# Column mean of an 8192 x 8192 matrix: other transfer sizes at both ends of the load stream, and a new assignment of PSUM banks

## Chip, cores, metric

One core of one Trainium2 chip. The metric is device time in microseconds (us), as the median of several executions; lower is better.

## The reference

```python
def setup_inputs():
    return {"x": np.random.randn(8192, 8192).astype(np.float32)}

def reference(x):
    return np.mean(x, axis=0)      # 8192 column means
```

The input is 268.4 MB of float32, the output 32 KB.

## The kernel before

The 8192 rows are 64 *slabs* of 128 rows, one row per partition. A transfer issued by GpSimd brings a slab from device memory and casts it to bfloat16 on the way. TensorE sums its 128 rows by multiplying with a column of ones, 512 columns (a *chunk*) per matmul, so 16 matmuls per slab, accumulating over all slabs in PSUM. At the end ScalarE (even chunks) and VectorE (odd chunks) multiply a finished chunk by 1/8192 and move it to a result row in SBUF (a *drain*), and the result row is stored.

Which bank a chunk accumulates in:

```python
    n_chunks = 16;  n_q = 2;  BANKS = 8;  QROWS = (0, 32, 64, 96)   # values for this shape
    def chunk_psum(c):
        b, q = c // n_q, c % n_q          # chunks 0,1 in bank 0; 2,3 in bank 1; ...
        return acc[QROWS[q] : QROWS[q] + 1, b * CHUNK : b * CHUNK + cw]
```

How the loads are cut. Slabs 0 to 59 come as 15 groups of four, slabs 60, 61 and 62 singly, and the last slab in nine narrow pieces. Groups and singles share two buffers of four slabs each; the last slab has one of its own.

```python
    slab_pool = tc.tile_pool(name="slab", bufs=2)
    bulk = n_slabs - 1
    # groups: (0,4) (4,4) ... (56,4), then (60,1) (61,1) (62,1)
    for g0, ns in groups:
        slab = slab_pool.tile([P, SPD * C], MM_DT)
        nc.gpsimd.dma_start(out=slab..., in_=x[g0 * P : (g0 + ns) * P, :]...)
        # 16 matmuls for each of the ns slabs
    ...
    last = slab_pool.tile([P, C], MM_DT)
    # pieces: [0,1] [2,3] ... [12,13] [14] [15]
    for pi, cs in enumerate(pieces):
        nc.gpsimd.dma_start(out=last[:, p0:pend], in_=row[:, p0:pend])
        # a matmul for each chunk of the piece, then its drain
        nc.sync.dma_start(out=out[p0:pend], in_=res[0:1, p0:pend])
```

The text above is the order in which the program is written. A scheduler, when the program is built, decides the order in which each engine issues its instructions, and the built order differs from it.

Of the kernel before, what the change touches and what calls it, by code (L numbers as in the profile page):

```python
# [1 line left out]

# [4 lines left out]



@with_exitstack  # L10
def kernel(
    ctx: ExitStack,
    tc: tile.TileContext,
    x: bass.AP,
    out: bass.AP,
):
    nc = tc.nc
    P = nc.NUM_PARTITIONS
    R, C = x.shape
    assert R % P == 0, "row count must be a multiple of 128"  # L20
    n_slabs = R // P

    MM_DT = mybir.dt.bfloat16
    CHUNK = 512
    BANKS = 8
    QROWS = (0, 32, 64, 96)
    n_chunks = (C + CHUNK - 1) // CHUNK
    n_q = (n_chunks + BANKS - 1) // BANKS
    assert n_q <= len(QROWS), "input too wide for a single pass"
    inv_r = 1.0 / float(R)  # L30

    const_pool = ctx.enter_context(tc.tile_pool(name="const", bufs=1))
    slab_pool = ctx.enter_context(tc.tile_pool(name="slab", bufs=2))
    psum_pool = ctx.enter_context(tc.tile_pool(name="acc", bufs=1, space=bass.MemoryType.PSUM))
    res_pool = ctx.enter_context(tc.tile_pool(name="res", bufs=1))

    ones_f32 = const_pool.tile([P, 1], mybir.dt.float32)
    nc.vector.memset(ones_f32, 1.0)  # L38
    ones = const_pool.tile([P, 1], MM_DT)
    nc.scalar.copy(out=ones, in_=ones_f32)  # L40

    acc = psum_pool.tile([P, BANKS * CHUNK], mybir.dt.float32)
    res = res_pool.tile([1, C], mybir.dt.float32)

    def chunk_psum(c):
        b, q = c // n_q, c % n_q
        cw = min(CHUNK, C - c * CHUNK)
        return acc[QROWS[q] : QROWS[q] + 1, b * CHUNK : b * CHUNK + cw]

    def chunk_cols(c):  # L50
        cw = min(CHUNK, C - c * CHUNK)
        return c * CHUNK, cw

    SPD = max(1, min(4, (8 << 20) // (P * C * 2)))
    TAIL_SINGLES = 3

    bulk = n_slabs - 1
    groups = []
    s0 = 0
    while s0 < max(0, bulk - TAIL_SINGLES):  # L60
        ns = min(SPD, bulk - TAIL_SINGLES - s0)
        groups.append((s0, ns))
        s0 += ns
    while s0 < bulk:
        groups.append((s0, 1))
        s0 += 1

    for g0, ns in groups:
        slab = slab_pool.tile([P, SPD * C], MM_DT)
        src = x[g0 * P : (g0 + ns) * P, :]  # L70
        if ns > 1:
            nc.gpsimd.dma_start(  # L72
                out=slab[:, : ns * C].rearrange("p (k c) -> p k c", c=C),
                in_=src.rearrange("(k p) c -> p k c", p=P),
            )
        else:
            nc.gpsimd.dma_start(out=slab[:, :C], in_=src)  # L77
        for k in range(ns):
            s = g0 + k
            for c in range(n_chunks):  # L80
                c0, cw = chunk_cols(c)
                nc.tensor.matmul(  # L82
                    out=chunk_psum(c),
                    lhsT=ones,
                    rhs=slab[:, k * C + c0 : k * C + c0 + cw],
                    start=(s == 0),
                    stop=False,
                )

    s = n_slabs - 1  # L90
    last = slab_pool.tile([P, C], MM_DT)
    row = x[s * P : (s + 1) * P, :]
    pieces = []
    for b in range(BANKS):
        cs = [c for c in range(b * n_q, min((b + 1) * n_q, n_chunks))]
        if not cs:
            continue
        if b == BANKS - 1 or (b + 1) * n_q >= n_chunks:
            pieces.extend([[c] for c in cs])
        else:  # L100
            pieces.append(cs)

    for pi, cs in enumerate(pieces):
        p0, _ = chunk_cols(cs[0])
        pend = chunk_cols(cs[-1])[0] + chunk_cols(cs[-1])[1]
        nc.gpsimd.dma_start(out=last[:, p0:pend], in_=row[:, p0:pend])  # L106
        for c in cs:
            c0, cw = chunk_cols(c)
            nc.tensor.matmul(  # L109
                out=chunk_psum(c),  # L110
                lhsT=ones,
                rhs=last[:, c0 : c0 + cw],
                start=(s == 0),
                stop=True,
            )
        for c in cs:
            c0, cw = chunk_cols(c)
            src_ap = chunk_psum(c)
            dst_ap = res[0:1, c0 : c0 + cw]
            if c % 2 == 0:  # L120
                nc.scalar.mul(out=dst_ap, in_=src_ap, mul=inv_r)  # L121
            else:
                nc.vector.tensor_scalar(  # L123
                    out=dst_ap,
                    in0=src_ap,
                    scalar1=inv_r,
                    scalar2=None,
                    op0=mybir.AluOpType.mult,
                )
        nc.sync.dma_start(out=out[p0:pend], in_=res[0:1, p0:pend])  # L130


# [1 line left out]
_INS = ['x']  # L134
_OUTS = [((8192,), 'float32')]


# [23 lines left out]
```

## Time and profile before

| | before |
|---|---|
| median time | 637.47 us (636.98 to 637.87, 5 runs) |
| span of the profiled execution | 635.0 us |
| TensorE busy | 148.7 us, 23% |
| device memory read | 268.44 MB, 423 GB/s over the span |
| last whole slab has landed | 623.4 us |
| from there to the end | 11.6 us |

First the profile page of the kernel before: the busy time of the engines, and the DMA and throughput rows of the table that cuts the span into 40 slices. A digit is the mean busy share of the 16 DMA engines in tenths; GB/s counts the bfloat16 bytes written, so device memory is read at twice that.

```profile
PE 148.7 (23%) x1024; PEld 51.4 (8%) x1024; DVE 4.9 (1%) x9; ACT 5.4 (1%) x10; POOL 17.8 (3%) x31
...
DMA  8999999999999999999999999999999999999992
GB/s 178 219 215 215 215 215 219 220 219 218 215 215 215 216 220 220 220 215 215 215 215 220 218 220 218 215 215 215 216 220 221 218 216 215 215 215 217 211 217 59
```

The loads keep the DMA engines busy from the first slice to the last but one, and no compute engine is near full. Only the ends are open to question, above all the last slice, where the rate falls to 59 GB/s.

Now the timeline of the kernel before near its end: start, duration, engine, source line, operation, output and input, how many merged; in brackets the idle time ahead and what ended it. First what GpSimd (POOL) issues; L77 is a whole slab, L106 a narrow piece of the last slab.

```profile
556.41 0.54 POOL L77 DMA_DIRECT2D slab<-in_x_dram  x1 [37.38 <-PE acc L82]
556.94 3.20 POOL L106 DMA_DIRECT2D last<-in_x_dram  x6
585.88 0.53 POOL L106 DMA_DIRECT2D last<-in_x_dram  x1 [25.74 <-DMA slab<-in_x_dram]
595.79 0.53 POOL L77 DMA_DIRECT2D slab<-in_x_dram  x1 [9.38 <-DMA slab<-in_x_dram]
597.50 0.53 POOL L77 DMA_DIRECT2D slab<-in_x_dram  x1 [1.18 <-PE acc L82]
598.03 0.53 POOL L106 DMA_DIRECT2D last<-in_x_dram  x1
599.33 0.53 POOL L106 DMA_DIRECT2D last<-in_x_dram  x1 [0.77 <-DMA last<-in_x_dram]
```

Seven of the nine narrow pieces are issued ahead of the last two whole slabs. The first of those two, by the view, waited last for the landing of the slab before it, the second for TensorE to give back a buffer (L77 waits for L82). The waits for a landing come from the built program, which hands its loads eight semaphores in turn: with eight loads under way, GpSimd issues the next one only when an earlier one has landed.

So seven narrow pieces land early (the seventh at 604.0 us), and a whole slab lands near the end, at 623.4 us. The page gives the median time from issue to landing of the two narrow pieces behind it:

```profile
last<-in_x_dram POOLq DMA_DIRECT2D x2, 128.0 KB, 25.7
```

The rest of that timeline, from that slab's landing on (weight loads left out):

```profile
623.43 3.31 PE L82 MATMUL acc<-slab,ones 128*1 128x512 bf16 x16 [6.10 <-DMA slab<-in_x_dram]
...
626.58 1.89 PE L109 MATMUL acc<-last,ones 128*1 128x512 bf16 x15
627.00 3.92 ACT L121 ACTIVATE res<-acc 1x512 f32<-1x512 f32 x8 [624.78 <-PE acc L109]
627.62 4.88 DVE L123 TENSOR_SCALAR res<-acc 1x512 f32<-1x512 f32 x8 [626.75 <-ACT res L121]
628.33 4.42 SPq L130 DMA_DIRECT2D out_dram<-res  x9
```

All 16 drains stand behind the whole slab: no chunk is complete before that slab's matmuls. VectorE's eight drains end at 632.5 us and the execution ends at 635.0 us.

### The profile page before, as it was taken

How to read it: one execution, taken by the hardware profiler on the slowest of the kernel's cores; microseconds unless marked ns; L12 is line 12 of the kernel's file. 1: busy time of each engine (PE TensorE's matmuls, PEld its weight loads, DVE VectorE, ACT ScalarE, POOL GpSimd, SP SyncE). 2: the span in 40 equal slices, each digit the busy share in tenths (PEclk: the TensorE clock that was granted, in tenths of full speed). 3: DMA queues.
4: the chain of work that ended last, by engine and by line, in shares of the span. 5: the costliest groups of instructions: out<-in, count | busy, mean ns of one | idle time of the engine just before them, and what ended most of it. 6: DMA issues, size and time to landing. Idle time of an engine off the chain costs nothing.

```text
span 635.0 us, 2169 instructions
## 1 busy us (share of the span) xinstructions
PE 148.7 (23%) x1024; PEld 51.4 (8%) x1024; DVE 4.9 (1%) x9; ACT 5.4 (1%) x10; POOL 17.8 (3%) x31
## 2 busy tenths in 40 slices
PE   0022060310604004060140502305041060501523
PEld 0010020100201001020010100102010020100200
DVE  0000000000000000000000000000000000000003
ACT  0000000000000000000000000000000000000002
POOL 1000000000000000000000000000000000020100
PEclk9997575575756658565585755757567575665957
DMA  8999999999999999999999999999999999999992
GB/s 178 219 215 215 215 215 219 220 219 218 215 215 215 216 220 220 220 215 215 215 215 220 218 220 218 215 215 215 216 220 221 218 216 215 215 215 217 211 217 59
DMA packets 9674, 134.38 MB, mean 212 GB/s; under 512 B 441, under 2 KB 697, under 8 KB 1602
## 3 DMA queue, kind: packets, MB, share of 16 engines
q0 software_dynamic: 9648, 134.22, 99.4%
q8 instruction: 8, 0.13, 0.1%
q1 hardware_dynamic: 18, 0.03, 0.0%
HBM read 268.44 MB, written 0.03 MB: 423 GB/s over the span
## 4 chain that ended last, share of the span: by engine, by line
another core or an unknown queue 60%; PE 21%; DMA 17%; DVE 1%; issue 0%; DVEq 0%; ACT 0%; POOLq 0%
PE acc L82 21%; DMA slab<-in_x_dram 17%; DVE res L123 1%; DVEq L156 0%; ACT res L121 0%; PE acc L109 0%; POOLq L145 0%
## 5 line engine op out<-in xcount | busy, mean ns | idle before, releaser
L82 PE MATMUL acc<-slab,ones 128*1 128x512 bf16 x1008 | 146.6, 461 | 480.1 <-DMA slab<-in_x_dram 480.1
L82 PEld LDWEIGHTS <-ones 128*1 128x1 bf16 x1008 | 50.7, 97 | 575.3 <-issue 532.2
L72 POOL DMA_DIRECT2D slab<-in_x_dram x15 | 11.3, 751 | 507.3 <-PE acc L82 506.5
L123 DVE TENSOR_SCALAR res<-acc 1x512 f32<-1x512 f32 x8 | 4.9, 673 | 626.8 <-ACT res L121 626.8
L121 ACT ACTIVATE res<-acc 1x512 f32<-1x512 f32 x8 | 3.9, 572 | 624.8 <-PE acc L109 624.8
L106 POOL DMA_DIRECT2D last<-in_x_dram x9 | 4.8, 553 | 26.5 <-DMA slab<-in_x_dram 25.7
L77 POOL DMA_DIRECT2D slab<-in_x_dram x3 | 1.6, 532 | 47.9 <-PE acc L82 38.6
L109 PE MATMUL acc<-last,ones 128*1 128x512 bf16 x16 | 2.3, 379 | 2.5 <-ACT res L121 2.5
L40 ACT ACT_TABLE_LOAD x1 | 1.3, 1283 | 0.7 <-PEq L145 0.7
L109 PEld LDWEIGHTS <-ones 128*1 128x1 bf16 x16 | 0.7, 84 | 1.2 <-issue 0.3
L40 ACT CAST ones<-ones_f 128x1 bf16<-128x1 f32 x1 | 0.2, 193 | 0.0
L145 POOL MEMSET const-float32-0.0<- 128x1 f32 x1 | 0.1, 98 | 0.2 <-issue 0.2
L145 POOL MEMSET const-bfloat16-1.0<- 128x1 bf16 x1 | 0.1, 101 | 0.0
L145 POOL MEMSET const-float32-1.0<- 128x1 f32 x1 | 0.1, 98 | 0.0
L145 POOL MEMSET const-uint8-127<- 128x1 uint8 x1 | 0.1, 98 | 0.0
L38 DVE MEMSET ones_f<- 128x1 f32 x1 | 0.1, 59 | 0.8 <-PEq L145 0.8
## 6 DMA issues: line engine op xcount, KB each, us to landing
slab<-in_x_dram POOLq DMA_DIRECT2D x15, 8192.0 KB, 68.0
slab<-in_x_dram POOLq DMA_DIRECT2D x3, 2048.0 KB, 25.9
last<-in_x_dram POOLq DMA_DIRECT2D x7, 256.0 KB, 41.1
last<-in_x_dram POOLq DMA_DIRECT2D x2, 128.0 KB, 25.7
out_dram<-res SPq DMA_DIRECT2D x7, 4.0 KB
out_dram<-res SPq DMA_DIRECT2D x2, 2.0 KB
```

The source lines that it names most:

```text
L38: nc.vector.memset(ones_f32, 1.0)
L40: nc.scalar.copy(out=ones, in_=ones_f32)
L72: nc.gpsimd.dma_start(out=slab[:, : ns * C].rearrange("p (k c) -> p k c", c=C), in_=src.rearrange("(k p) c -> p k c", p=P),)
L77: nc.gpsimd.dma_start(out=slab[:, :C], in_=src)
L82: nc.tensor.matmul(out=chunk_psum(c), lhsT=ones, rhs=slab[:, k * C + c0 : k * C + c0 + cw], start=(s == 0), stop=False,)
L106: nc.gpsimd.dma_start(out=last[:, p0:pend], in_=row[:, p0:pend])
L109: nc.tensor.matmul(out=chunk_psum(c), lhsT=ones, rhs=last[:, c0 : c0 + cw], start=(s == 0), stop=True,)
L121: nc.scalar.mul(out=dst_ap, in_=src_ap, mul=inv_r)
L123: nc.vector.tensor_scalar(out=dst_ap, in0=src_ap, scalar1=inv_r, scalar2=None, op0=mybir.AluOpType.mult,)
L145: nc = _bacc.Bacc("TRN2", target_bir_lowering=False, num_devices=1)
```

## The change

The intent is to leave less work for the end, when the last transfers land. The diff, cut to its core (constants are written with their values; the unused ones it introduces, and code that only moved into helper functions, are left out):

```diff
     def chunk_psum(c):
-        b, q = c // n_q, c % n_q
+        q = c % n_q
+        b = (c // n_q + q * BANKS // n_q) % BANKS
...
-    SPD = 4;  TAIL_SINGLES = 3
-    bulk = n_slabs - 1
-    # 15 groups of four, then slabs 60, 61, 62 singly
+    SPD = 4;  FIRST_SMALL = 2
+    bulk_end = n_slabs - 2
+    # slabs 0 and 1 singly, then 15 groups of four
...
-    last = slab_pool.tile([P, C], MM_DT)
-    # nine narrow pieces of slab 63: load, matmuls, drains, store of each
+    with tc.manual_schedule():
+        # last 2 slabs by blocks of columns, in the other slab buffer
+        g0 = n_slabs - 2
+        slab = slab_pool.tile([P, SPD * C], MM_DT)
+        sv = slab[:, : 2 * C].rearrange("p (k c) -> p k c", c=C)
+        xv = x[g0 * P : n_slabs * P, :].rearrange("(k p) c -> p k c", p=P)
+        for a, b in [(0, 8), (8, 12), (12, 14), (14, 16)]:
+            p0, pend = a * CHUNK, b * CHUNK
+            nc.gpsimd.dma_start(out=sv[:, :, p0:pend], in_=xv[:, :, p0:pend])
+        for a, b in [(0, 8), (8, 12), (12, 14), (14, 16)]:
+            p0, pend = a * CHUNK, b * CHUNK
+            for k in range(2):
+                slab_matmuls(slab[:, k * C : (k + 1) * C], g0 + k, range(a, b))
+            for c in range(a, b):
+                drain(c, c % 2)
+            nc.sync.dma_start(out=out[p0:pend], in_=res[0:1, p0:pend])
```

There are three parts: the *head* (two single slabs first), the *banks* (an even chunk and the odd chunk after it no longer share a bank), and the *tail* (the last two slabs together, cut by columns, with the order of issue written out instead of left to the scheduler).

More of the change, by code (lines that the diff above doesn't have):

```diff
@@ L1 @@
+import os
 from contextlib import ExitStack
@@ L30 @@
     inv_r = 1.0 / float(R)
+    SPD = int(os.environ.get("CM_SPD", "4"))
+    SING = int(os.environ.get("CM_SING", "3"))
+    NARROW = int(os.environ.get("CM_NARROW", "2"))
+    FIRST_SMALL = int(os.environ.get("CM_FIRST", "2"))
     const_pool = ctx.enter_context(tc.tile_pool(name="const", bufs=1))
@@ L52, in chunk_cols, with slab_matmuls, drain @@
         return c * CHUNK, cw
-    SPD = max(1, min(4, (8 << 20) // (P * C * 2)))
-    TAIL_SINGLES = 3
-    bulk = n_slabs - 1
-    groups = []
-    s0 = 0
-    while s0 < max(0, bulk - TAIL_SINGLES):
-        ns = min(SPD, bulk - TAIL_SINGLES - s0)
+    def slab_matmuls(slab_ap, s, chunks, npass=0):
+        for c in chunks:
+            c0, cw = chunk_cols(c)
+            nc.tensor.matmul(
+                out=chunk_psum(c),
+                lhsT=ones,
+                rhs=slab_ap[:, c0 : c0 + cw],
+                start=(s == 0),
+                stop=(s == n_slabs - 1),
+            )
+    def drain(c, engine):
+        c0, cw = chunk_cols(c)
+        src_ap = chunk_psum(c)
+        dst_ap = res[0:1, c0 : c0 + cw]
+        if engine == 0:
+            nc.scalar.mul(out=dst_ap, in_=src_ap, mul=inv_r)
+        else:
+            nc.vector.tensor_scalar(
+                out=dst_ap,
+                in0=src_ap,
+                scalar1=inv_r,
+                scalar2=None,
+                op0=mybir.AluOpType.mult,
+            )
+    bulk_end = n_slabs - 2
+    head_end = min(FIRST_SMALL, bulk_end)
+    groups = []
+    for s in range(head_end):
+        groups.append((s, 1))
+    s0 = head_end
+    while s0 < bulk_end:
+        ns = min(SPD, bulk_end - s0)
         groups.append((s0, ns))
         s0 += ns
-    while s0 < bulk:
-        groups.append((s0, 1))
-        s0 += 1
     for g0, ns in groups:
@@ L78 @@
         for k in range(ns):
-            s = g0 + k
-            for c in range(n_chunks):
-                c0, cw = chunk_cols(c)
-                nc.tensor.matmul(
-                    out=chunk_psum(c),
-                    lhsT=ones,
-                    rhs=slab[:, k * C + c0 : k * C + c0 + cw],
-                    start=(s == 0),
-                    stop=False,
-                )
-    s = n_slabs - 1
-    last = slab_pool.tile([P, C], MM_DT)
-    row = x[s * P : (s + 1) * P, :]
-    pieces = []
@@ L94 @@
-    for b in range(BANKS):
-        cs = [c for c in range(b * n_q, min((b + 1) * n_q, n_chunks))]
-        if not cs:
-            continue
-        if b == BANKS - 1 or (b + 1) * n_q >= n_chunks:
-            pieces.extend([[c] for c in cs])
-        else:
-            pieces.append(cs)
-    for pi, cs in enumerate(pieces):
-        p0, _ = chunk_cols(cs[0])
-        pend = chunk_cols(cs[-1])[0] + chunk_cols(cs[-1])[1]
-        nc.gpsimd.dma_start(out=last[:, p0:pend], in_=row[:, p0:pend])
-        for c in cs:
-            c0, cw = chunk_cols(c)
-            nc.tensor.matmul(
-                out=chunk_psum(c),
-                lhsT=ones,
-                rhs=last[:, c0 : c0 + cw],
-                start=(s == 0),
-                stop=True,
-            )
-        for c in cs:
-            c0, cw = chunk_cols(c)
-            src_ap = chunk_psum(c)
-            dst_ap = res[0:1, c0 : c0 + cw]
-            if c % 2 == 0:
-                nc.scalar.mul(out=dst_ap, in_=src_ap, mul=inv_r)
-            else:
-                nc.vector.tensor_scalar(
-                    out=dst_ap,
-                    in0=src_ap,
-                    scalar1=inv_r,
-                    scalar2=None,
-                    op0=mybir.AluOpType.mult,
-                )
-        nc.sync.dma_start(out=out[p0:pend], in_=res[0:1, p0:pend])
@@ new lines @@
+            slab_matmuls(slab[:, k * C : (k + 1) * C], g0 + k, range(n_chunks))
+    with tc.manual_schedule():
[13 more added lines that the diff above has]
+            nc.sync.dma_start(out=out[p0:pend], in_=res[0:1, p0:pend])
```

## The prediction

> **What bounds the kernel now.** The load stream. In the slice table the DMA row is 8 or 9 tenths in every slice but the last; TensorE is busy 23%, the other engines at most 3%. The chain of waits shows the 8192 KB groups landing at 42.9, 81.6, ... 585.6 us: 38.8 us each, for 16.8 MB of float32, 433 GB/s. The Trainium skill ("DMA: Bandwidth & Descriptors", Where 436 GB/s comes from) gives the fabric ceiling as 435 GB/s; this trace agrees, so the stream itself can't get shorter. Sixteen group-equivalents at 38.8 us, plus 4.1 us before the first could flow (42.9 - 38.8), put the last byte at about 624.4 us, with any grouping.
>
> **What the kernel before wastes.** Only the ends.
> - Start: bytes move from about 2.4 us. TensorE waits until 42.9 us, but has slack: 64 matmuls take 8.6 to 9.9 us of each 38.8.
> - Tail: the last whole slab lands at 623.4 us. The timeline then shows its 16 matmuls (3.3 us), those of the last row block, VectorE's eight drains from 627.6 to 632.5 us (4.9 us; ScalarE's eight from 627.0), the last store issue at 632.5 and the end at 635.0 us: 11.6 us after the landing. The narrow pieces of the last slab were issued ahead and landed before or with that whole slab (the last two issued at 598.0 and 599.3 us, about 25.7 us to landing), so narrowing them bought nothing: everything waits for the whole slab.
>
> **What the change does.**
> 1. Tail (critical path): the last two slabs come together, in column blocks of 8, 4, 2 and 2 chunks, all issued while the last big group still streams. A block carries both slabs, so its columns are finished when it lands. The last landing comes some 4.85 us after the one before (a quarter of a slab pair's 19.4), and earlier drains fit in that. After it remain: 4 matmuls, 0.9 us at the timeline's 0.43 us per pair; one ScalarE drain beside one VectorE drain in different banks (572 and 673 ns; start about 0.1); the store issue (0.1) and the same 2.5 us to the end. Sum 4.2 us against 11.6.
> 2. Head: two single slabs instead of a group of four. TensorE starts at about 14 us; off the critical path, worth about 0. The risk: the next group is issued only when slab 0 has been summed, about 14 + 3.5 us, while slab 1 streams until about 23.5 us. Some 5 us of slack: no gap expected.
> 3. Bank rotation: neighbouring matmuls in different banks. TensorE is not the bottleneck; about 0, apart from letting the two last drains overlap.
>
> **Prediction.** Last landing 624.3 us, span about 628.5 us, saving 6.5 us; the measured time is 2.5 us above the span (637.47 against 635.0). Predicted 631.0 us, 80% range 628.8 to 633.4, about 1% faster. Chances: faster by over 2% 0.03, within 2% 0.94, slower by over 2% 0.03.
>
> **What would show it.** Step 1: the chain of waits ends with a slab landing at 623.5 to 625, then about 4 us; two drains only after it; DMA row near full until then. Step 2: first matmul near 14 us, no hole in DMA between 15 and 30 us. Step 3: the matmul group's busy time may change, the total doesn't. Landings stay 38.8 us apart.
>
> **What would make it wrong.** A DMA gap near 20 us; slower transfers of the column blocks (row pieces of 4 to 16 KB of float32; the before's 1024-column pieces ran at about 209 GB/s against 215 in the windows); the last drains waiting for one another; or the group rate shifting by 1% (6 us), which would hide or double the gain.

## The result

| | before | after |
|---|---|---|
| median time | 637.42 us (636.95 to 637.87, 13 runs) | 630.29 us (629.85 to 630.57, 7 runs) |
| ratio, 95% interval | | 0.9889 (0.9879 to 0.9899) |
| span of the profiled execution | 635.0 us | 628.4 us |
| last whole slab or last block has landed | 623.4 us | 624.4 us |
| from there to the end | 11.6 us | 4.0 us |
| last load of any size has landed | 624.7 us | 624.4 us |

A ratio is the mean time of one kernel's fast runs over that of the other's fast runs of the same rounds, so it is not quite the ratio of the medians quoted. The kernel is 1.1% faster, which is within 2%. The two spans differ by 6.6 us, which is 7.6 us less after the landing that the drains waited for, less 1.0 us by which that landing came later. The stream of loads itself ended at about the same time in both.

From the page of the changed kernel, the same two rows as above (TensorE is busy for 149.2 us, 24%):

```profile
DMA  8999999999999999999999999999999999999997
GB/s 181 213 217 215 217 217 217 217 216 217 217 216 218 216 217 217 217 217 216 218 217 217 217 215 217 217 217 217 216 218 217 217 217 217 217 215 218 217 214 144
```

The middle has not changed. The last slice moves 144 GB/s instead of 59: it holds fewer idle microseconds.

The timeline of the changed kernel near its end (L119 is the issue of the four blocks; weight loads and parts in between left out):

```profile
575.04 2.81 POOL L119 DMA_DIRECT2D slab<-in_x_dram  x4 [37.37 <-PE acc L64]
...
621.98 1.01 PE L64 MATMUL acc<-slab,ones 128*1 128x512 bf16 x4 [1.42 <-DMA slab<-in_x_dram]
623.03 0.59 ACT L77 ACTIVATE res<-acc 1x512 f32<-1x512 f32 x1 [1.61 <-PE acc L64]
623.14 0.68 DVE L79 TENSOR_SCALAR res<-acc 1x512 f32<-1x512 f32 x1 [1.38 <-PE acc L64]
624.43 1.02 PE L64 MATMUL acc<-slab,ones 128*1 128x512 bf16 x4 [1.43 <-DMA slab<-in_x_dram]
...
625.48 0.59 ACT L77 ACTIVATE res<-acc 1x512 f32<-1x512 f32 x1 [1.86 <-PE acc L64]
625.59 0.68 DVE L79 TENSOR_SCALAR res<-acc 1x512 f32<-1x512 f32 x1 [1.77 <-PE acc L64]
```

All four blocks are issued by 577.9 us, 27 us before the last full group lands (604.8 us). The last two blocks land 2.45 us apart. After the last landing there are 4 matmuls, two drains side by side, and the store; VectorE ends at 626.3 us and the execution at 628.4 us.

The head in the timeline of the changed kernel: TensorE starts at 13.8 us instead of 42.9, and the next group is issued 5.7 us before slab 1 has landed (0.04 us ahead of its first matmul).

```profile
13.82 3.58 PE L64 MATMUL acc<-slab,ones 128*1 128x512 bf16 x16 [13.82 <-DMA slab<-in_x_dram]
...
17.70 0.75 POOL L102 DMA_DIRECT2D slab<-in_x_dram  x1 [15.23 <-PE acc L64]
23.48 3.36 PE L64 MATMUL acc<-slab,ones 128*1 128x512 bf16 x16 [6.08 <-DMA slab<-in_x_dram]
```

The table of stretches shows no hole there: 210 and 211 GB/s between 10 and 20 and between 20 and 30 us, in both kernels alike.

### The profile page after: what moved, and what is told of

It reads as the page before. It is cut to its first block, busy times and chain, and to the rows that moved or that the text cites. A ratio compares the mean times of both kernels' runs of the same rounds, so it can differ in the third digit from the quotient of the medians.

```text
span 628.4 us, 2168 instructions
## 1 busy us (share of the span) xinstructions
PE 149.2 (24%) x1024; PEld 51.1 (8%) x1024; DVE 5.2 (1%) x9; ACT 5.7 (1%) x10; POOL 15.4 (2%) x25
## 4 chain that ended last, share of the span: by engine, by line
another core or an unknown queue 61%; PE 21%; DMA 17%; issue 0%; POOL 0%; POOLq 0%; DVE 0%; DVEq 0%
PE acc L64 21%; DMA slab<-in_x_dram 17%; POOL slab L119 0%; POOLq L152 0%; DVE res L79 0%; DVEq L79 0%; POOLq L141 0%
## 5 line engine op out<-in xcount | busy, mean ns | idle before, releaser
L64 PE MATMUL acc<-slab,ones 128*1 128x512 bf16 x1024 | 149.2, 461 | 476.3 <-DMA slab<-in_x_dram 476.3
L102 POOL DMA_DIRECT2D slab<-in_x_dram x15 | 11.1, 741 | 524.1 <-PE acc L64 524.1
L119 POOL DMA_DIRECT2D slab<-in_x_dram x4 | 2.8, 710 | 37.4 <-PE acc L64 37.4
L107 POOL DMA_DIRECT2D slab<-in_x_dram x2 | 1.2, 622 | 0.8 <-POOLq L141 0.8
```

The costliest lines, as they stand in the source:

```text
L64: nc.tensor.matmul(out=chunk_psum(c), lhsT=ones, rhs=slab_ap[:, c0 : c0 + cw], start=(s == 0), stop=(s == n_slabs - 1),)
L102: nc.gpsimd.dma_start(out=slab[:, : ns * C].rearrange("p (k c) -> p k c", c=C), in_=src.rearrange("(k p) c -> p k c", p=P),)
L107: nc.gpsimd.dma_start(out=slab[:, :C], in_=src)
L119: nc.gpsimd.dma_start(out=sv[:, :, p0:pend], in_=xv[:, :, p0:pend])
```

## The experiments

The number fitted. That doesn't show that the reasons did, so each of the three parts was run alone, and then the sizes and orders on which the reasoning rests were changed. Four kernels, then four, then three, shared a chip and the runs of the kernel before, whose median was 637.42, 637.46 and 637.41 us. The theory: the stream of loads ends at about 624.4 us whatever one does, and the time is that plus the work that only a late landing sets free. The rivals give the gain to TensorE's earlier start, to the banks, or to having fewer transfers.

### e1: the tail alone

Edit, from the changed kernel: the other two parts are undone.

```diff
-    FIRST_SMALL = 2
+    FIRST_SMALL = 0        # groups of four from slab 0 (the last group has two)
...
-        b = (c // n_q + q * BANKS // n_q) % BANKS
+        b = c // n_q
```

> The kernel before with only the new tail (groups of four from the start, banks as before). Theory (the tail is all of the gain): last landing at about 624.4 us as in the changed kernel, but the last two drains share a bank and run one after the other, 0.6 us more, so 630.9 us (630.3 to 631.5). Rival (the early start of TensorE with single slabs, or the bank rotation, carries part of the 7.1 us): 632 us or more.

Measured: 630.74 us (630.68 to 630.93), ratio 0.9894 (0.9881 to 0.9908). The theory's number. The last lines of its timeline:

```profile
624.58 1.01 PE L63 MATMUL acc<-slab,ones 128*1 128x512 bf16 x4 [1.45 <-DMA slab<-in_x_dram]
625.64 0.59 ACT L76 ACTIVATE res<-acc 1x512 f32<-1x512 f32 x1 [1.88 <-PE acc L63]
626.26 0.68 DVE L78 TENSOR_SCALAR res<-acc 1x512 f32<-1x512 f32 x1 [1.78 <-ACT res L76]
```

VectorE's drain now waits for ScalarE's (0.62 us behind it, not 0.11), because chunks 14 and 15 share a bank. That is what the rotation is worth in the new tail; run e10 below, which differs from e1 in the banks alone, is 0.48 us faster.

### e2: the banks alone

Edit, from the kernel before: only the two lines of `chunk_psum` in the diff above.

> The kernel before with only the rotated banks. Theory: only the 0.6 us by which VectorE's first drain waited for ScalarE's in the same bank can go, so 636.8 to 637.4 us. Rival (bank sharing between drains and matmuls is what makes the tail 11.6 us long): 632 to 635 us.

Measured: 636.45 us (636.38 to 637.12), ratio 0.9987 (0.9973 to 1.0). That is 0.35 us below the range of the theory, and far from the rival's. The median of the kernel before is 0.97 us higher, the profiled executions differ by the expected 0.60 us (636.98 and 636.38), and the interval of the ratio reaches from nothing to 1.7 us: the size of so small a gain isn't settled. In the timeline VectorE's drains start at 626.97 us, 0.04 us after ScalarE's; in the kernel before at 627.62 us, 0.62 us after. The drains themselves still take 4.9 us.

### e3: the old tail, issued in another order

Edit, from the kernel before: slabs 60 to 62 and the nine pieces of slab 63 go into the four parts of one slab buffer. The same transfers of the same sizes, but once that one buffer is free no load of the tail waits for TensorE, and the build issues the whole slabs first and then the pieces in column order.

```diff
-    # slabs 60, 61, 62: one shared slab buffer each; slab 63: its own tile "last"
+    tail = slab_pool.tile([P, SPD * C], MM_DT, name="slab")
+    for s in range(tail0, bulk):                       # slabs 60, 61, 62
+        k = s - tail0
+        nc.gpsimd.dma_start(out=tail[:, k * C : (k + 1) * C], in_=x[s * P : (s + 1) * P, :])
+        # its 16 matmuls
...
-    last = slab_pool.tile([P, C], MM_DT)
+    last = tail[:, 3 * C : 4 * C]                      # the nine narrow pieces, as before
```

> The kernel before with its own three whole slabs and nine narrow pieces, but all in one slab buffer, so that they are issued in column order with no whole slab behind the narrow pieces. Theory (the narrow pieces before bought nothing because a whole slab landed last): the last to land is one 512-column piece at about 624.5 to 625 us, then 1 matmul, 1 drain and the store, 3.3 to 4 us: 630.0 to 631.2 us. Rival (pairing two slabs per block, or fewer DMAs, is what the gain needs): 634 us or more.

Measured: 631.09 us (630.99 to 631.26), ratio 0.9899 (0.9886 to 0.9913). The same three whole slabs and nine narrow pieces, with the old banks and the old head, give 6.3 of the 7.1 us. The last whole slab now lands at 614.7 us and the narrow pieces behind it, the last but one at 624.15 us and the last at 624.8 us. From its timeline, the matmuls of the last whole slab and of the last chunk:

```profile
614.77 3.58 PE L94 MATMUL acc<-slab,ones 128*1 128x512 bf16 x16 [6.11 <-DMA slab<-in_x_dram]
...
625.46 0.59 PE L121 MATMUL acc<-slab,ones 128*1 128x512 bf16 x1 [0.67 <-ACT res L133]
```

So the narrow pieces of the kernel before were a sound idea that was spoilt by the whole slabs queued behind seven of them; blocks of two slabs and fewer transfers are not what most of the gain needs. Most of the missing 0.8 us goes to a wait that the old banks bring: the last chunk's matmul starts 0.66 us after its piece has landed, since ScalarE is still draining chunk 14 from the same bank. In e5, with the same loads and rotated banks, it starts at once (624.76 us, 0.05 us after the landing), and 630.27 us were measured.

### e4: one wide block

Edit, from the changed kernel: both lists of blocks.

```diff
-        for a, b in [(0, 8), (8, 12), (12, 14), (14, 16)]:
+        for a, b in [(0, 16)]:
```

> The changed kernel with one block of 16 chunks in place of blocks of 8, 4, 2 and 2. Theory (what counts is how much work is left after the last landing): landing at 624.4 us as before, then 32 matmuls of which half must pass before a chunk is finished (3.4 us), eight VectorE drains of 0.62 us (5.0 us), store and end 2.3 us: about 11 us after the landing in place of 4.0, 637.3 us (636 to 638). Rival (early issue of all the last loads and the bank rotation carry the gain, not the narrow blocks): 630 to 633 us.

Measured: 639.62 us (638.99 to 639.99), ratio 1.0032 (1.0019 to 1.0044). Early issue and rotated banks without narrow blocks are slower than the kernel before, so the rival falls: what is left to do after the last landing decides. The theory's size was off, however, by 2.3 us. The timeline:

```profile
624.27 5.47 PE L64 MATMUL acc<-slab,ones 128*1 128x512 bf16 x32 [10.99 <-DMA slab<-in_x_dram]
629.13 4.89 DVE L79 TENSOR_SCALAR res<-acc 1x512 f32<-1x512 f32 x8 [628.26 <-PE acc L64]
```

The landing is right, the drains' length is right, but the first drain starts 4.9 us after the landing and not 3.4, and from VectorE's last drain (634.0 us) to the end of the span (637.2 us) it takes 3.2 us and not 2.3. Run e11 follows up the first of the two.

### e5 and e6: a candidate for something better, beside the changed kernel

Edit of e5, from e3: the rotated banks, and the tail kept in program order, so that only one chunk is left when the last piece lands.

```diff
-        b, q = c // n_q, c % n_q
+        q = c % n_q
+        b = (c // n_q + q * BANKS // n_q) % BANKS
...
+    with tc.manual_schedule():
         # the tail of e3, one level deeper
```

> The kernel of e3 (own slab buffer for the tail, whole slabs first, then narrow pieces of the last slab) with the rotated banks as well and the tail kept in program order. Theory: after the last landing (about 624.2 us) 1 matmul (0.6 to the drain), one VectorE drain (0.68), store and end (2.2): 3.5 us in place of the changed kernel's 4.0, so 629.4 to 630.0 us, 0.3 to 0.9 us under the changed kernel in the same rounds. Rival (nine narrow transfers cost the stream more than four blocks do, landing later): equal to it or slower, 630.3 to 631.5 us.

e6 is the changed kernel again.

> The changed kernel once more, for comparison in the same rounds: 630.3 us (629.9 to 630.7) by any theory.

Measured: e5 630.27 us (630.18 to 630.72), e6 630.30 us (630.26 to 630.43). They tie, and the hoped-for 0.3 to 0.9 us isn't there. The profiles show why. From the last landing to the end of VectorE's drain e5 takes 1.35 us and the changed kernel 1.88 us, so the 0.5 us that the smaller last piece was to save are there. They are lost in two other places. The last piece landed at 624.7 us, 0.5 us later than assumed: the assumed 624.2 us was the landing of the last but one in e3. And from VectorE's end to the end of the span e5 takes 2.45 us, the changed kernel 2.1 us.

Both differences run through all profiles (one execution of each run). The last load lands between 624.63 and 624.81 us in the six kernels with nine narrow pieces (before, e2, e3, e5, e7, e9), and between 624.15 and 624.63 us in the five with the four blocks (the changed kernel twice, e1, e8, e10). That is 0.3 us on average and speaks for the rival. From VectorE's end it takes 2.45 to 2.50 us with nine stores of the result, 2.08 to 2.13 us with four and 3.1 to 3.2 us with one (e4, e11). Why either is so was not tested.

### e7: the head alone

Edit, from the kernel before:

```diff
     groups = []
-    s0 = 0
+    groups = [(0, 1), (1, 1)]
+    s0 = 2
     while s0 < max(0, bulk - TAIL_SINGLES):
```

> The kernel before with only the new head: slabs 0 and 1 as single transfers. Theory (TensorE's late start was slack): first matmul at about 14 us in place of 43 us, and the same end, 637.0 to 637.9 us. Rival (the early start is worth something at the end): 636 us or less. Rival (the single slabs leave the queue dry near 20 us): 639 us or more.

Measured: 632.24 us (631.21 to 633.26), ratio 0.992 (0.9907 to 0.9932). A plain miss: alone, the head gains 5.2 us (6.2 us in the profiled execution, the fastest of the five), though TensorE's late start is slack. Two lines added at the first slab must have done something at the other end. What GpSimd issues near the end of e7 (L78 a whole slab, L107 a narrow piece):

```profile
576.45 0.57 POOL L78 DMA_DIRECT2D slab<-in_x_dram  x1 [39.10 <-PE acc L83]
591.20 0.54 POOL L78 DMA_DIRECT2D slab<-in_x_dram  x1 [14.18 <-PE acc L83]
599.02 0.53 POOL L78 DMA_DIRECT2D slab<-in_x_dram  x1 [7.28 <-PE acc L83]
599.54 3.19 POOL L107 DMA_DIRECT2D last<-in_x_dram  x6
605.41 0.53 POOL L107 DMA_DIRECT2D last<-in_x_dram  x1 [2.68 <-DMA slab<-in_x_dram]
615.07 0.53 POOL L107 DMA_DIRECT2D last<-in_x_dram  x1 [9.13 <-DMA slab<-in_x_dram]
616.27 0.53 POOL L107 DMA_DIRECT2D last<-in_x_dram  x1 [0.68 <-DMA last<-in_x_dram]
```

Set beside the same list of the kernel before, the order has turned round: all three whole slabs first, then all nine narrow pieces. The built program has this order already, before any run; it is also the order in which the source is written. With two slabs taken at the front, the last group of the bulk has two slabs and not four, and the scheduler orders the tail otherwise. The last whole slab is summed from 614.8 us on, as in e3, and the last narrow piece lands at 624.8 us. This gave a new theory (the gain is the order), tested in e9.

### e8: a sixth of TensorE's work

Edit, from the changed kernel; the result is wrong:

```diff
-            slab_matmuls(slab..., g0 + k, range(n_chunks))
+            slab_matmuls(slab..., g0 + k, range(n_chunks) if g0 + k == 0 else range(2))
```

> The changed kernel with the same loads, but slabs 1 to 61 summed in 2 of 16 chunks only (so the result is wrong on purpose): TensorE does about a sixth of the matmuls. Theory (the stream bounds it, and a slab buffer is freed long before the queue runs dry): landings still 38.7 us apart, 629.7 to 630.7 us. Rival (the wait of the loads for TensorE's release of a buffer costs something per group): buffers freed some 7 us earlier in each of 15 groups, 628 us or less.

Measured: 629.91 us (629.85 to 630.12). GpSimd could issue the third group of four at 64.3 us instead of about 72.1, and the last block still landed at 624.15 us. The stream doesn't wait for TensorE in the bulk.

### e9: the new head with the old order of the tail

Edit, from e7: the tail is written in an order that the scheduler may not change, the one that the kernel before had.

```diff
+    with tc.manual_schedule():
+        for i, sl in enumerate(singles):               # slabs 60, 61, 62
+            slab = slab_pool.tile([P, SPD * C], MM_DT, name="slab")
+            nc.gpsimd.dma_start(out=slab[:, :C], in_=x[sl * P : (sl + 1) * P, :])
+            if i == 0:
+                for cs in pieces[:7]:
+                    load_piece(cs)
+            # 16 matmuls
+        for cs in pieces[7:]:
+            load_piece(cs)
+        # matmuls, drains and stores of the nine pieces, as before
```

> The kernel of e7 (new head, old tail), but the transfers of the tail are issued in the order that the kernel before had: one whole slab, seven narrow pieces, two whole slabs, two narrow pieces. Theory (the head alone gained 5.2 us only because the build then issued the narrow pieces behind all the whole slabs): the last whole slab lands at about 623.5 to 624 us again with all the drains behind it, 637.0 to 638.2 us. Rival (the early start of TensorE itself, or the shift of the groups by two slabs, is worth the 5 us): 631 to 633.5 us.

Measured: 637.38 us (637.02 to 637.72), ratio 1.0 (0.9987 to 1.0013). The whole gain of e7 is gone. GpSimd's issues, and then the landing (L100 and L108 belong to whole slabs, L96 to narrow pieces):

```profile
576.18 0.57 POOL L100 DMA_DIRECT2D slab<-in_x_dram  x1 [39.10 <-PE acc L80]
576.74 3.20 POOL L96 DMA_DIRECT2D last<-in_x_dram  x6
...
599.16 0.53 POOL L100 DMA_DIRECT2D slab<-in_x_dram  x1 [2.86 <-PE acc L108]
599.68 1.07 POOL L96 DMA_DIRECT2D last<-in_x_dram  x2
...
623.49 3.58 PE L108 MATMUL acc<-slab,ones 128*1 128x512 bf16 x16 [6.18 <-DMA slab<-in_x_dram]
```

The head, the cut of the tail and the banks are those of e7; the order of issue is that of the kernel before, and so is the time.

### e10: the changed kernel without the head

Edit: `FIRST_SMALL = 0` in the changed kernel.

> The changed kernel with the new head undone (groups of four from the first slab, a group of two ahead of the tail), new tail and rotated banks kept. Theory (behind the new tail the head is worth nothing): 629.9 to 630.8 us. Rival (the head is worth part of its 5.2 us here too): 632 us or more.

Measured: 630.26 us (629.83 to 630.74), ratio 0.9889 (0.9874 to 0.9904), the changed kernel's 630.29 again. Behind a tail whose order is fixed, the head is worth nothing.

### e11: the wide block with the old banks

Edit: e4 with the old `chunk_psum`.

> The kernel of e4 (one block of 16 chunks, which missed its forecast by 2 us: the first drains started 4.9 us after the landing, not 3.4) with the banks as before. Theory (with rotated banks chunk 0 shares its bank with chunk 9 and chunk 1 with chunk 8, so the first drains wait for the 25th and 26th matmul): with the pairs 0 and 1, 2 and 3 in one bank, the first ScalarE drain starts behind the 18th matmul, about 4.0 us after the landing, VectorE's 0.6 us behind it; 638.6 to 639.5 us. Rival (the drains were late for another reason): the first drain again at about 4.9 us.

Measured: 638.70 us (638.38 to 639.21), ratio 1.0023 (1.001 to 1.0035). The last lines of its timeline:

```profile
624.25 5.50 PE L63 MATMUL acc<-slab,ones 128*1 128x512 bf16 x32 [10.95 <-DMA slab<-in_x_dram]
628.28 3.93 ACT L76 ACTIVATE res<-acc 1x512 f32<-1x512 f32 x8 [626.06 <-PE acc L63]
628.90 4.89 DVE L78 TENSOR_SCALAR res<-acc 1x512 f32<-1x512 f32 x8 [628.04 <-ACT res L76]
```

ScalarE's first drain starts 4.0 us after the landing and VectorE's 0.62 us later, as expected. The chain of waits counts the matmuls between the landing and the first drain on it (start, duration, what); first e4's, then e11's:

```profile
624.27 4.87 PE acc L64 x24
```

```profile
624.25 4.01 PE acc L63 x18
```

(For e4 the view counts 24, one fewer than the forecast of e11.) So a drain waits for both chunks of its bank, in either assignment, and e4's forecast had left that out. With the old banks VectorE starts 4.65 us after the landing, behind 18 matmuls and ScalarE's first drain; with rotated ones 4.86 us, since chunk 0 shares its bank with chunk 9 and chunk 1 with chunk 8, whose matmuls in a wide block come late. Of e4's miss of 2.3 us, then, 1.5 us are the later start of VectorE's drains, of which the rotation is only 0.2 us, and 0.9 us the longer end. In the changed kernel the two chunks of the last block share a bank with chunks finished long before, so only the gain is left.

## Why the prediction was right, and where it wasn't

**The stream sets the end: right.** It predicted the last landing at 624.3 us; it came at 624.4 us. In all thirteen profiles, with other cuts, orders, banks and a sixth of the matmuls, the last load landed between 624.15 and 624.81 us. What the prediction had wrong is that the narrow pieces of the kernel before "landed before or with that whole slab": the last two landed 0.7 and 1.35 us after it. This changes nothing in the sum, since TensorE was busy with the slab until then.

**What remains after it: the mechanism right, and 4.0 us against 4.2 forecast, in part by luck.** The terms: from the landing to the start of VectorE's drain 1.2 us, where 0.9 for the 4 matmuls and a start of 0.1 were forecast; VectorE's drain 0.68; from its end to the end of the span 2.1 us, where 0.1 and 2.5 were forecast. So one term was 0.2 us too small and the other 0.5 us too large: the prediction took over the end of a kernel with nine stores, and with four it is shorter (e5). e3 and e4 show the mechanism from two sides: with only narrow pieces in the last 9 us 6.3 us are gained, with a wide block landing last 2.2 us are lost.

**The spacing of the last blocks: wrong by a factor of two.** The prediction said that "the last landing comes some 4.85 us after the one before (a quarter of a slab pair's 19.4)". Two chunks of 16 are an eighth, 2.4 us, and 2.45 us was measured. The conclusion held, with less room than claimed: VectorE's drain of the block before ended at 623.8 us, 0.6 us before the last landing.

**The head "worth about 0": right inside this change, wrong alone.** The reason given was right, since TensorE's early start buys nothing (e9, e10). The step that failed is that the head was judged by what it does at the start. With the old tail it changed the order in which the build issues the last transfers, and that was worth 5.2 us (e7), all of which goes when the old order is put back (e9). The parts' gains therefore don't add: head alone 5.2, tail alone 6.7, banks alone 0.6 to 1.0, all three together 7.1 us. Head and tail remove the same wait.

**The banks "about 0, apart from letting the two last drains overlap": right.** In the new tail it is 0.5 us of start time (e1's 0.62 against 0.11 us).

**Measured time above the span: mis-sized.** 2.5 us was taken from the median time and the span of the profiled execution, which was a quick one. From the same execution it is 2.0 us, and in the changed kernel 1.8 us. That is why 631.0 was forecast and 630.29 measured, with the span right to 0.1 us.

What stays open: e7's five runs spread over 2.0 us (631.2 to 633.3) where the other kernels' spread over 0.2 to 1.0. In e7 the slower executions are also those with the lower mean granted clock of TensorE (0.667 for the fastest, 0.614 for the two slowest), which the runs of the changed kernel don't show; whether that is the cause was not tested. Why the scheduler chooses the one order or the other was not studied either; only the two orders and their times are shown.

## What to carry to other kernels

In a kernel that is bound by its load stream, ask of each of the last landings how much work only that one sets free: here 11.6 us to the end behind a whole slab, 4.0 us behind two chunks of two slabs. Cutting the last transfers small helps only if the large ones have landed well before them, so read the order of issue from the built program or the timeline, not from the source, and fix it where it matters. And before crediting a part of a change with its gain, run it with the others absent and present, since two parts can remove the same wait.

## What the Trainium skill lacked or had wrong

- "DMA: Bandwidth & Descriptors", Where 436 GB/s comes from: its fabric ceiling of 435 GB/s agrees with this trace, 433 GB/s of float32 read per group (16.8 MB each 38.8 us). But the page derives it from SBUF's ports, and on that side these casting loads write only half as many bytes, some 217 GB/s of bfloat16. The page doesn't say on which side a casting load is to be counted, so that the ports are the limit here is not shown. The warning in the same section that for transfers between device memory and SBUF the memory side, about 358 GB/s, binds is not met in this program, which runs on one core: 427 GB/s over the whole span of the changed kernel. "HBM Reference", Specifications, has it right (about 425 GB/s for a core streaming alone).
- "PSUM — Partial Sum Buffer", PSUM bank collisions raise a hardware error: it quotes that two engines may access one bank at the same time if they are in different quadrants. The kernel before drains its even and odd chunks from different quadrants (partitions 0 and 32) of one bank, and its VectorE drains nevertheless wait for ScalarE's, 0.62 us behind (0.04 us in e2, with other banks). The wait stands in the built program, so it doesn't contradict the page; the page tells of added dependencies within one bank and quadrant, and not that a build may also add one across quadrants. Draining without that wait in one bank was not tried.
- No page says that the built order of transfers can differ from the written one, and that this can decide the time: 632.24 against 637.38 us for the same transfers in two orders (e7, e9).
